# Counting the experts in use: sums of the dense gates on GpSimd, or products of one-hots on TensorE

## The chip, the cores and the metric

The kernel runs on one core of a Trainium2 chip. Its time is device microseconds for one execution, the median of several. Five engines work side by side, each through its own list of instructions in order: TensorE (PE; its weight loads are shown as PEld), VectorE (DVE), ScalarE (ACT), GpSimd (POOL) and SyncE (SP), which issues transfers. They wait for each other by semaphores. TensorE writes to PSUM, in banks of 128x512 fp32; SBUF holds the rest.

## The reference, cut to what matters

One layer works on 256 latent tokens of width 2048 (with 256 context tokens that only the first half of the layer reads): a token mixer, and then an expert layer (PEER), which is where the change lies.

```
q  = (hb @ w_q).reshape(128, 8 heads, 2, 128)
s1, s2 = q[:, :, 0] . k1, q[:, :, 1] . k2              # 128 scores each
v1, i1 = top_k(s1, 16);  v2, i2 = top_k(s2, 16)
sc, flat = top_k(v1[:, None] + v2[None, :], 16)        # 16 pairs for each token and head
idx = e1 * 128 + e2                                    # one of 16384 experts
g   = softmax(sc)
act = gelu(hb . u_tab[idx])
out = sum over the 128 (head, k) of (g * act) * v_tab[idx]
```

Each token picks 8 x 16 experts. An expert is one row of u_tab and one of v_tab, of 2048 fp32 each.

## The kernel before, in words

**Stages.** Up to about 600 us: modulation, norm, the mixer and its output projection, then the queries and scores of the expert layer. From there to about 1380 us runs the u stage: 128 steps (`u_step`, L1181), one for each tile of 128 experts of u_tab. All 16384 experts are computed for all 256 tokens. A step has 16 pairs of matmuls (L1188, L1190) into one of four banks. Each u tile comes by DMA and is split into a high and a low part, in two halves of 1024 columns: ScalarE rounds (L255), VectorE subtracts (L256). Five half buffers let these splits be made two tiles ahead of their step. From the eighth step on ScalarE copies the bank out (L1203), GpSimd adds its two halves (L1204), and in the next step ScalarE applies the GeLU (L1209) and stores the activations to DRAM. Then comes the v stage: rows of v_tab in use are gathered by index and multiplied.

**What is done beneath the u stage.** `beneath` (L1160) is a generator of small pieces of work. In each u step `fill` takes pieces from it until their given costs use up a budget of 3000; what is left over or overdrawn is carried on. So the order on each engine is settled by the program, not by what is free at the time. In a u step it is: the splits, the u matmuls, the pieces, the GeLU of the step before, the copy out. The pieces are routing (top-k and softmax), `gates`, `places` and `make_list`.

**Gates.** The gates are spread into a dense table G[e2, e1, token]: expert (e1, e2) has partition e2 and column e1. This is done in 32 blocks of 8 tokens (TB); for tokens of a half (NB = 16 blocks). Partitions hold the 128 (head, k) slots. For each block VectorE makes one-hots of e2 (OHA) and of e1 (both L1025), and multiplies those of e1 by the gate's high and low fp16 parts (L1034). A block later TensorE multiplies, for each of 8 tokens, the e2 one-hot by both scaled e1 one-hots (L1057, two matmuls into banks 6 and 7: G for 4 tokens in each), and the e2 one-hot by the plain e1 one-hot (L1054), which counts how often each expert is picked: bank 4 for the first 128 tokens, bank 5 for the others, accumulated over 16 blocks. A block later again `keep` has ScalarE copy banks 6 and 7 to the dense table GC in SBUF (L1067, four tokens each). GC holds 64 tokens in 128 columns of 64, so the four tokens of one copy are 128 runs of four numbers. Finished tables go to DRAM (`agd`) in pieces.

**Places.** After the last block VectorE compares both counts with 0.5 (L1093, L1094), which tells which experts the first half, the second or both use. From this the list of v rows is made.

Of the kernel before, what the change touches and what calls it, by code (L numbers as in the profile page):

```python
# [14 lines left out]
ALU = mybir.AluOpType  # L15
AX = mybir.AxisListType

P = 128
# [32 lines left out]
def layer_kernel(ctx: ExitStack, tc: tile.TileContext, I, out, dbg=None):  # L51
    nc = tc.nc
    V, S, G, TE = nc.vector, nc.scalar, nc.gpsimd, nc.tensor
# [11 lines left out]
    pb = [psum.tile([P, 512], F32, name=f"bank{i}") for i in range(8)]  # L65

    def q_(off, n):
        assert O_Q + off + n <= N_F
        return fa[:, O_Q + off:O_Q + off + n]
# [793 lines left out]
    TB = 8  # L863
    NB = P // TB
# [5 lines left out]
    GC = [a.rearrange("p (c t) -> p c t", t=HT) for a in (fb[:, 0:8192], q_(0, 8192))]  # L870
# [4 lines left out]
    PM, PJ = q_(11264, 64).bitcast(BF), q_(11328, 64).bitcast(BF)  # L875
    VAL = q_(11392, 128).bitcast(F16).rearrange("p (n q) -> p n q", q=2)
    PT = [q_(11520, 128)] + [q_(12288 + 128 * i, 128) for i in range(4)]
    STAGE = [q_(12032, 256), q_(14976, 256), dg2]
    eg = q_(14336, 512)
    E1T, E2T = eg[:, 0:128].bitcast(BF), eg[:, 128:256].bitcast(BF)  # L880
# [131 lines left out]
    def list_tables():  # L1012
# [5 lines left out]
        V.tensor_scalar(VAL[:, :, 1], iota_f, 0.0, pidx, op0=ALU.mult, op1=ALU.add)  # L1018
        V.memset(PT[0], 0.0)
        S.dma_start(agd[0:1, :].rearrange("a (b c) -> (a b) c", c=P), PT[0][0:4, :])  # L1020
        yield 1000


    def one_hot(dst, numbers, n):
        V.tensor_tensor(dst, iota_b[:, 0:n].unsqueeze(1).to_broadcast([P, TB, n]),  # L1025
                        numbers.unsqueeze(2).to_broadcast([P, TB, n]), op=ALU.is_equal)

    def pair(b, n):
        return (OHB[b % 2][:, 0:TB * n].rearrange("p (t j) -> p t j", t=TB),
                OHG[b % 2][:, 0:2 * TB * n].rearrange("p (t q j) -> p t q j", t=TB, q=2))  # L1030

    def scaled(b, factors, n):
        oj, og = pair(b, n)
        V.tensor_tensor(og, oj.unsqueeze(2).to_broadcast([P, TB, 2, n]),  # L1034
                        factors.unsqueeze(3).to_broadcast([P, TB, 2, n]), op=ALU.mult)
# [5 lines left out]
    def store_piece(eng):  # L1041
        if pieces:
            c, x = pieces.pop(0)
            cs = slice(8 * x, 8 * x + 8)
            eng.dma_start(ag4[cs, :, c // 2, 1, (c % 2) * HT:(c % 2 + 1) * HT].rearrange("c e i -> e c i"),
                          GC[c % 2][:, cs, :])

    def gates():
        def products(b):
            counts = pb[4 + b // NB][:, 0:P]  # L1050
            oj, og = pair(b, P)
            for i in range(TB):
                oa = OHA[b % 2][:, i, :]
                TE.matmul(counts, oa, oj[:, i, :], start=b % NB == 0 and i == 0,  # L1054
                          stop=b % NB == NB - 1 and i == TB - 1, skip_group_check=True)
                for q in range(2):
                    TE.matmul(pb[6 + i // 4][:, (i % 4) * P:(i % 4 + 1) * P], oa, og[:, i, q, :],  # L1057
                              start=i % 4 == 0 and q == 0, stop=q == 1, skip_group_check=True)

        def keep(b):  # L1060
            c, o = divmod(b, HT // TB)
            if o == 0:
                while pieces and pieces[0][0] < c - 1:
                    store_piece(S)
            for x in range(2):
                tl = slice(o * TB + 4 * x, o * TB + 4 * x + 4)
                S.activation(GC[c % 2][:, :, tl], pb[6 + x].rearrange("p (t j) -> p j t", j=P), AF.Copy,  # L1067
                             scale=1.0 / GSC)
            if o == HT // TB - 1:
                pieces.extend((c, x) for x in range(16))  # L1070

        for b in range(2 * NB + 2):
            sl = slice(b * TB, (b + 1) * TB)
            if b < 2 * NB:
                one_hot(OHA[b % 2], E2T[:, sl], P)
                one_hot(pair(b, P)[0], E1T[:, sl], P)
            yield 2300
            if b < 2 * NB:
                scaled(b, GT[:, sl, :], P)
            if b > 1:  # L1080
                keep(b - 2)
            if 0 < b <= 2 * NB:
                products(b - 1)
            yield 2400
# [3 lines left out]
    def places():  # L1088
        flat = [o.rearrange("p t i -> p (t i)")[:, 0:P].bitcast(BF) for o in OHA]
        u0, u1 = flat[0], flat[1]  # L1090
        part = [x[:, 0:P].bitcast(BF) for x in (OHB[0], OHB[1], OHG[1])]
        one, tot, inc, pos = PT[0], PT[1], PT[2], PT[3]
        V.tensor_scalar(u0, pb[4][:, 0:P], 0.5, None, op0=ALU.is_gt)  # L1093
        V.tensor_scalar(u1, pb[5][:, 0:P], 0.5, None, op0=ALU.is_gt)  # L1094
        V.tensor_tensor(part[1], u0, u1, op=ALU.mult)
        V.tensor_tensor(part[0], u0, part[1], op=ALU.subtract)
        V.tensor_tensor(part[2], u1, part[1], op=ALU.subtract)
        yield 1500
        for x in range(3):
            TE.matmul(pb[6][:, x * P:(x + 1) * P], LT, part[x], start=x == 0, stop=True, skip_group_check=True)  # L1100
            TE.matmul(pb[7][:, x * P:(x + 1) * P], ONES, part[x], start=x == 0, stop=True, skip_group_check=True)
        V.memset(one, 1.0)
        V.memset(pos, BIG)
        yield 500

        for x in range(3):
            V.tensor_copy(tot, pb[7][:, x * P:(x + 1) * P])
            V.tensor_tensor_scan(inc, one, tot, 0.0, op0=ALU.mult, op1=ALU.add)
            V.tensor_tensor(tot, inc, tot, op=ALU.subtract)
            V.tensor_tensor(tot, pb[6][:, x * P:(x + 1) * P], tot, op=ALU.add)  # L1110
            if x == 0:
                V.tensor_scalar(flag[:, 0:1], inc[:, P - 1:P], float(N_A * P), None, op0=ALU.is_gt)
                V.tensor_scalar(PT[4], tot, float(N_A * P) - 0.5, BIG, op0=ALU.is_gt, op1=ALU.mult)
                V.tensor_tensor(tot, tot, PT[4], op=ALU.add)
            else:
                base = float(N_A * P) if x == 1 else flag[:, 1:2]
                V.tensor_scalar(tot, tot, base, None, op0=ALU.add)
                V.tensor_scalar(flag[:, x:x + 1], inc[:, P - 1:P], base, None, op0=ALU.add)
            V.scalar_tensor_tensor(tot, tot, -BIG, part[x], op0=ALU.add, op1=ALU.mult)
            V.tensor_tensor(pos, pos, tot, op=ALU.add)  # L1120
            yield 2200
        V.tensor_scalar(flag[:, 1:2], flag[:, 1:2], float(N_0 * P), None, op0=ALU.is_gt)
        V.tensor_scalar(flag[:, 2:3], flag[:, 2:3], float(N_L * P), None, op0=ALU.is_gt)
        G.dma_start(ptab.rearrange("(p c) a -> p (c a)", p=P), pos)
        pu, pj = PT[4].bitcast(U32), PT[0].bitcast(U32)
        V.tensor_copy(pu, pos)
        V.tensor_scalar(pj, pu, 7, None, op0=ALU.logical_shift_right)
        V.tensor_copy(PJ, pj)
        V.tensor_scalar(pu, pu, P - 1, None, op0=ALU.bitwise_and)
        V.tensor_copy(PM, pu)  # L1130
        yield 2500
# [28 lines left out]
    def beneath():  # L1160
        yield from routing()
        yield from list_tables()
        yield from gates()
        yield from places()
        yield from make_list()
        while pieces:
            yield 0
        for n in range(N_RAW):
            yield from (0 for _ in starts(NU - 16 + 3 * n))
            gather(n)  # L1170
            yield 100
# [9 lines left out]
    def u_step(n, fill):  # L1181
# [15 lines left out]
        u_out(n - 1)  # L1197
        st = STAGE[n % 3]
        if n < 8:
# [6 lines left out]
    def u_out(n):  # L1206
        if n >= 0:
            st = STAGE[n % 3]
            S.activation(st, st, AF.Gelu_apprx_tanh)  # L1209
            S.dma_start(ag4[n, :, :, 0, :], st.rearrange("p (t i) -> p t i", t=2))  # L1210
# [80 lines left out]
    with tc.If(more > 0):  # L1291
# [23 lines left out]
        for t in range(2):  # L1315
# [9 lines left out]
            for q in range(4):  # L1325
                c = slice(q * 512, (q + 1) * 512)
# [163 lines left out]
```

## Time and profile before

| | |
|---|---|
| time, median of 3 runs (lowest to highest) | 1791.05 us (1789.89 to 1794.6) |
| the profiled execution: its time, its span | 1794.17 us, 1792.4 us |
| mean granted TensorE clock | 0.982 of full speed |
| busy share: TensorE, VectorE, ScalarE, GpSimd | 95%, 75%, 51%, 22% |
| u stage with gate products | 778 to 1106 us |

Busy time of an engine adds up its instructions; an instruction that has been issued and waits for something inside its engine is shown as busy. "L256" is line 256 of the kernel. In a group `out<-in` are the buffers by the program's names (`fa`, `fb`: large fp32 buffers in SBUF; `ra`: the rounded parts; `bank`: PSUM), followed by partitions x elements, type and the number of instructions. A wait is shown with the engine, buffer and line that ended it.

### The profile page before, as it was taken

The numbers are of one execution on the slowest core, as the hardware profiler recorded it, in microseconds if no ns is written. First come the engines' busy times: TensorE is split into PE (matmuls) and PEld (weight loads), VectorE is DVE, ScalarE is ACT, GpSimd is POOL, SyncE is SP. The second block draws the span as 40 slices with busy tenths as digits, with TensorE's granted clock in tenths as the row PEclk, the third lists the DMA queues.
The fourth block names the chain that finished last, engine by engine and source line by source line (L and its number), as shares of the span: only waits on it lengthen the run. The fifth ranks groups of instructions, "written<-read, shape, count | busy, mean of one in ns | idle before, by whom it ended". The sixth has DMA issues, their size and how long they took to land.

```text
span 1792.4 us, 26487 instructions
## 1 busy us (share of the span) xinstructions
PE 1707.9 (95%) x10313; PEld 1422.4 (79%) x10313; DVE 1340.4 (75%) x1812; ACT 922.0 (51%) x1232; POOL 401.5 (22%) x341
## 2 busy tenths in 40 slices
PE   4999999999999999999999999999998799999995
PEld 0778566788799888888888888888887688888884
DVE  1347697687788999898888886988443577777776
ACT  5223666643543455555555555444454465656554
POOL 0000000000100002222222221212112565656652
PEclk8999999999999999999999999999999899999997
DMA  9877778888797656655787888865675789888881
GB/s 394 335 307 281 297 274 323 329 322 299 291 338 283 242 202 215 209 187 184 220 236 227 226 242 235 260 216 189 213 276 189 247 307 350 309 304 307 305 315 59
DMA packets 166266, 472.43 MB, mean 264 GB/s; under 512 B 76692, under 2 KB 109640, under 8 KB 115960
## 3 DMA queue, kind: packets, MB, share of 16 engines
q1 hardware_dynamic: 92544, 316.17, 50.3%
q0 software_dynamic: 21120, 128.68, 20.3%
q10 hardware_dynamic: 52472, 25.84, 5.0%
q8 instruction: 82, 1.34, 0.3%
q14 instruction: 48, 0.39, 0.1%
HBM read 432.81 MB, written 37.83 MB: 263 GB/s over the span
## 4 chain that ended last, share of the span: by engine, by line
PE 80%; DVE 11%; DMA 5%; issue 2%; ACT 2%; POOL 0%; SPq 0%; DVEq 0%; POOLq 0%; ACTq 0%
PE bank L1188 23%; PE bank L284 13%; PE bank L286 12%; PE bank L285 12%; PE bank L1190 12%; DVE ra L256 4%; DMA fa<-in_wm_a_dram 2%; DMA fa<-in_wm_c_dram 2%; PE bank L1057 2%; PE bank L364 1%; PE bank L309 1%; DVE fa L290 1%; DVE fa L942 1%; PE bank L527 1%; DVE fa L940 1%
## 5 line engine op out<-in xcount | busy, mean ns | idle before, releaser
L256 DVE TENSOR_TENSOR ra<-fa,ra 128x1024 fp32r<-128x1024 f32 x564 | 702.0, 1259 | 291.9 <-ACT ra L255 286.2
L255 ACT ACTIVATE ra<-fa 128x1024 fp32r<-128x1024 f32 x564 | 591.3, 1057 | 473.7 <-PE bank L1188 187.3
L1188 PE MATMUL bank<-ra 128*128 128x512 f32 x2048 | 731.9, 401 | 0.0
L1190 PE MATMUL bank<-ra 128*128 128x256 f32 x2048 | 576.9, 282 | 5.1 <-DVE ra L256 5.0
L284 PE MATMUL bank<-ra 128*128 128x512 f32 (+1 forms) x1364 | 475.0, 348 | 17.9 <-ACT ra L1229 16.8
L286 PE MATMUL bank<-ra 128*128 128x512 f32 (+1 forms) x1364 | 468.2, 343 | 5.4 <-DVE ra L1234 4.5
L285 PE MATMUL bank<-ra 128*128 128x512 f32 (+1 forms) x1364 | 467.8, 343 | 1.4 <-DVE ra L256 1.4
L1188 PEld LDWEIGHTS bank<-ra 128*128 128x128 f32 x2048 | 385.8, 188 | 92.6 <-ACT ra L255 0.2
L1190 PEld LDWEIGHTS bank<-ra 128*128 128x128 f32 x2048 | 387.7, 189 | 8.5 <-DVE ra L256 8.4
L284 PEld LDWEIGHTS bank<-ra 128*128 128x128 f32 x1364 | 261.8, 192 | 76.7 <-issue 25.8
L1204 POOL TENSOR_TENSOR fa<-fa 128x256 f32<-128x256 f32 x120 | 150.9, 1258 | 724.2 <-ACT fa L1203 724.1
L286 PEld LDWEIGHTS bank<-ra 128*128 128x128 f32 x1364 | 261.5, 192 | 36.7 <-DVE ra L1234 6.5
L285 PEld LDWEIGHTS bank<-ra 128*128 128x128 f32 x1364 | 261.8, 192 | 32.1 <-DVE ra L256 3.1
L1203 ACT ACTIVATE fa<-bank 128x512 f32<-128x512 f32 x120 | 71.8, 598 | 145.8 <-PE bank L1190 139.8
L898 POOL DMA_INDIRECT fa<-agd,fa x92 | 128.3, 1395 | 39.1 <-issue 26.5
L898 POOL DMA_INDIRECT fa<-in_peer_v_dram,fa x92 | 97.4, 1058 | 119.8 <-DVE ra L256 80.1
L1025 DVE TENSOR_TENSOR fa<-fa 128x1024 f16<-128x1024 bf16 x96 | 113.5, 1223 | 0.0
L1034 DVE TENSOR_TENSOR fa<-fa 128x2048 f16<-128x2048 f16 (+1 forms) x48 | 109.2, 2275 | 0.8
L290 DVE SCALAR_TENSOR_TENSOR fa<-fa 128x2048 f32<-128x2048 f32 x32 | 72.9, 2284 | 0.0
L1209 ACT ACTIVATE fa<-fa 128x256 f32<-128x256 f32 x128 | 52.0, 407 | 33.7 <-DVE fa L1201 25.6
L364 PE MATMUL bank<-fa 128*2 128x512 f32 x256 | 39.6, 711 | 25.5 <-DMA fa<-in_wm_a_dram 17.4
L1229 ACT ACTIVATE ra<-fa 128x128 fp32r<-128x128 f32 x92 | 32.4, 352 | 50.9 <-DVE fa L1220 50.7
(264 smaller groups left out, 1168.1 us busy)
## 6 DMA issues: line engine op xcount, KB each, us to landing
fa<-in_peer_u_dram SPq DMA_DIRECT2D x128, 1024.0 KB, 5.1
fa<-in_wm_a_dram SPq DMA_DIRECT2D x32, 1024.0 KB, 7.8
fa<-in_wm_c_dram SPq DMA_DIRECT2D x32, 1024.0 KB, 6.8
fa<-in_wm_d_dram SPq DMA_DIRECT2D x32, 1024.0 KB, 6.8
fa<-in_w_in_dram SPq DMA_DIRECT2D x24, 1024.0 KB, 4.9
fa<-in_w_out_dram SPq DMA_DIRECT2D x16, 1024.0 KB, 6.7
fa<-in_wq_dram SPq DMA_DIRECT2D x16, 1024.0 KB, 7.4
agd<-fa ACTq DMA_DIRECT2D x128, 128.0 KB, 2.4
```

The costliest lines, as they stand in the source:

```text
L255: S.activation(h, x, AF.Copy)
L256: V.tensor_tensor(l, x, h.bitcast(F32), op=ALU.subtract)
L284: TE.matmul(dst, wh, mh, start=first, stop=False, skip_group_check=skip)
L285: TE.matmul(dst, wh, ml, start=False, stop=False, skip_group_check=skip)
L286: TE.matmul(dst, wl, mh, start=False, stop=last, skip_group_check=skip)
L290: V.scalar_tensor_tensor(junk, w, 1.0, s, op0=ALU.mult, op1=ALU.mult, accum_out=dst)
L898: G.indirect_dma_start(out=dst, out_offset=None, in_=src, in_offset=bass.IndirectOffsetOnAxis(ap=idx, axis=0), bounds_check=bound, oob_is_ ...
L1025: V.tensor_tensor(dst, iota_b[:, 0:n].unsqueeze(1).to_broadcast([P, TB, n]), numbers.unsqueeze(2).to_broadcast([P, TB, n]), op=ALU.is_equal)
L1034: V.tensor_tensor(og, oj.unsqueeze(2).to_broadcast([P, TB, 2, n]), factors.unsqueeze(3).to_broadcast([P, TB, 2, n]), op=ALU.mult)
L1188: TE.matmul(bank, h[:, es], H2[:, k, :, :].rearrange("p z t -> p (z t)"), start=k == 0, stop=False, skip_group_check=True)
L1190: TE.matmul(bank[:, 0:T], l[:, es], HH[:, k, :], start=False, stop=k == KD - 1, skip_group_check=True)
L1204: G.tensor_tensor(st, HALVES[:, 0:T], HALVES[:, T:2 * T], op=ALU.add)
```

## The change

TensorE no longer counts. After each `keep` GpSimd adds the two freshly copied quarters of the dense table to a running sum SUMS (128 columns x 4), two additions of 128x512 for each block, one in the first block of each half. After the sixteenth block of a half VectorE reduces SUMS over its last axis to USED (128x128), and `places` compares USED with zero. A used expert has a positive gate. What is left of `places` and all other stages are unchanged, and lines move by up to 8.

```diff
+    SUMS = q_(12288, 512).rearrange("p (j t) -> p j t", t=4)
+    USED = [q_(11648 + 128 * i, 128) for i in range(2)]
...
         def products(b):
-            counts = pb[4 + b // NB][:, 0:P]
             oj, og = pair(b, P)
             for i in range(TB):
                 oa = OHA[b % 2][:, i, :]
-                TE.matmul(counts, oa, oj[:, i, :], start=b % NB == 0 and i == 0,
-                          stop=b % NB == NB - 1 and i == TB - 1, skip_group_check=True)
                 for q in range(2):
...
+            quarter = [GC[c % 2][:, :, o * TB + 4 * x:o * TB + 4 * x + 4] for x in range(2)]
+            if b % NB == 0:
+                G.tensor_tensor(SUMS, quarter[0], quarter[1], op=ALU.add)
+            else:
+                for x in range(2):
+                    G.tensor_tensor(SUMS, SUMS, quarter[x], op=ALU.add)
+            if b % NB == NB - 1:
+                V.tensor_reduce(USED[b // NB], SUMS, axis=AX.X, op=ALU.add)
...
-        V.tensor_scalar(u0, pb[4][:, 0:P], 0.5, None, op0=ALU.is_gt)
-        V.tensor_scalar(u1, pb[5][:, 0:P], 0.5, None, op0=ALU.is_gt)
+        V.tensor_scalar(u0, USED[0], 0.0, None, op0=ALU.is_gt)
+        V.tensor_scalar(u1, USED[1], 0.0, None, op0=ALU.is_gt)
```

TensorE at the first products, before (bank_78 takes the counts, bank_80 the gates):

```order
L1188 MATMUL bank_76<-ra 128x512
L1190 MATMUL bank_76<-ra 128x256
L1054 LDWEIGHTS fa
L1054 MATMUL bank_78<-fa 128x128
L1057 LDWEIGHTS fa
L1057 MATMUL bank_80<-fa 128x128
L1057 LDWEIGHTS fa
L1057 MATMUL bank_80<-fa 128x128
L1054 LDWEIGHTS fa
```

The same place now (u matmuls are L1196 and L1198, gate products L1056):

```order
L1196 MATMUL bank_76<-ra 128x512
L1198 MATMUL bank_76<-ra 128x256
L1056 LDWEIGHTS fa
L1056 MATMUL bank_80<-fa 128x128
L1056 LDWEIGHTS fa
L1056 MATMUL bank_80<-fa 128x128
L1056 LDWEIGHTS fa
```

A count went with its own weight load: three loads and three matmuls for each token have become two and two.

GpSimd's list in the u stage, before (L1204 is the addition of a u step):

```order
L1204 TENSOR_TENSOR fa<-fa 128x256
L726 DMA m5d<-fa 16x128
L1204 TENSOR_TENSOR fa<-fa 128x256 x18
L1013 IOTA fa 128x1
L1204 TENSOR_TENSOR fa<-fa 128x256 x57
L1124 DMA ptab<-fa 128x128
```

And now (L1212 is what L1204 was, L1071 and L1074 are the new additions):

```order
L1015 IOTA fa 128x1
L1212 TENSOR_TENSOR fa<-fa 128x256 x4
L1071 TENSOR_TENSOR fa<-fb 128x512
L1212 TENSOR_TENSOR fa<-fa 128x256 x2
L1074 TENSOR_TENSOR fa<-fa,fb 128x512 x2
L1212 TENSOR_TENSOR fa<-fa 128x256
L1074 TENSOR_TENSOR fa<-fa,fb 128x512 x2
L1212 TENSOR_TENSOR fa<-fa 128x256 x2
```

Two new additions stand ahead of the u step's own in each step that keeps a block.

VectorE at the end of the first half, now (L1027 one-hots, L1036 scaled one-hots, L256 splits; L1076 waits for GpSimd):

```order
L256 TENSOR_TENSOR ra<-fa,ra 128x1024 x2
L1027 TENSOR_TENSOR fa<-fa 128x1024 x2
L256 TENSOR_TENSOR ra<-fa,ra 128x1024 x2
L1036 TENSOR_TENSOR fa<-fa 128x2048
L1076 TENSOR_REDUCE fa<-fa 128x128
L256 TENSOR_TENSOR ra<-fa,ra 128x1024 x2
L1027 TENSOR_TENSOR fa<-fa 128x1024 x2
```

Apart from L1076, here and once more ahead of `places`, VectorE's list is what it was.

## Rows read from the trace of the kernel before

**Rows 1.** The page, busy us (share of the span) xinstructions.
```profile
PE 1707.9 (95%) x10313; PEld 1422.4 (79%) x10313; DVE 1340.4 (75%) x1812; ACT 922.0 (51%) x1232; POOL 401.5 (22%) x341
```
**Rows 2.** The page, chain that ended last, shares of the span by line.
```profile
PE bank L1188 23%; PE bank L284 13%; PE bank L286 12%; PE bank L285 12%; PE bank L1190 12%; DVE ra L256 4%; DMA fa<-in_wm_a_dram 2%; DMA fa<-in_wm_c_dram 2%; PE bank L1057 2%; PE bank L364 1%; PE bank L309 1%; DVE fa L290 1%; DVE fa L942 1%; PE bank L527 1%; DVE fa L940 1%
```
**Rows 3.** Stretches: length, busy of PE, PEld, DVE, ACT, POOL (x), PEclk, DMA, GB/s.
```profile
778.00:1091.00 313.00, 313.00 (x2270) 273.76 (x2269) 275.48 (x189) 167.48 (x250) 76.13 (x48) 1.00 0.76 220
1091.00:1106.00 15.00, 15.00 (x103) 13.10 (x102) 5.92 (x5) 8.90 (x14) 1.47 (x2) 1.00 0.86 233
```
**Rows 4.** Groups, 778 to 1106 us: xcount | busy us, mean ns | idle before.
```profile
L256 DVE TENSOR_TENSOR ra<-fa,ra 128x1024 fp32r<-128x1024 f32 x102 | 140.7, 1390 | 46.4 <-ACT ra L255 46.3
...
L1204 POOL TENSOR_TENSOR fa<-fa 128x256 f32<-128x256 f32 x50 | 77.6, 1552 | 249.2 <-ACT fa L1203 249.2
L1025 DVE TENSOR_TENSOR fa<-fa 128x1024 f16<-128x1024 bf16 x61 | 75.1, 1270 | 0.0
L1034 DVE TENSOR_TENSOR fa<-fa 128x2048 f16<-128x2048 f16 x31 | 74.4, 2399 | 0.2
```
**Rows 5.** VectorE's timeline in the u stage: start us, us, instruction.
```profile
817.89 2.29 DVE L1034 TENSOR_TENSOR fa<-fa 128x2048 f16<-128x2048 f16 x1
820.17 1.68 DVE L256 TENSOR_TENSOR ra<-fa,ra 128x1024 fp32r<-128x1024 f32 x1
```
**Rows 6.** GpSimd's timeline at the same time.
```profile
819.27 1.50 POOL L1204 TENSOR_TENSOR fa<-fa 128x256 f32<-128x256 f32 x1 [3.86 <-ACT fa L1203]
```
**Rows 7.** By line, whole span: ns min/median/max, first and last start us, forms.
```profile
L256 DVE TENSOR_TENSOR ra<-fa,ra x564: 1164/1225/1765, 37.7 to 1773.7; 128x1024 fp32r<-128x1024 f32 x188
L1025 DVE TENSOR_TENSOR fa<-fa x96: 909/1217/1762, 764.5 to 1247.5; 128x1024 f16<-128x1024 bf16 x80, 128x736 f16<-128x736 bf16 x16
L1034 DVE TENSOR_TENSOR fa<-fa x48: 1691/2285/2823, 770.1 to 1248.4; 128x2048 f16<-128x2048 f16 x32, 128x1472 f16<-128x1472 f16 x16
L776 DVE TENSOR_TENSOR fa<-bank,fa x8: 678/684/692, 469.4 to 479.1; 128x512 f32<-128x512 f32 x8
L777 POOL TENSOR_TENSOR fb<-fa,fb x4: 1283/1292/1296, 470.2 to 474.0; 128x512 f32<-128x512 f32 x4
L777 DVE TENSOR_TENSOR fb<-fa,fb x4: 692/692/1447, 474.4 to 479.8; 128x512 f32<-128x512 f32 x4
L1371 POOL TENSOR_TENSOR fb<-fb,fa x7: 1267/1277/1290, 1749.9 to 1782.6; 128x512 f32<-128x512 f32 x7
L1204 POOL TENSOR_TENSOR fa<-fa x120: 727/1470/2683, 653.2 to 1384.6; 128x256 f32<-128x256 f32 x120
```
**Rows 8.** Timelines of GpSimd and VectorE, 468 to 482 us.
```profile
470.24 5.04 POOL L777 TENSOR_TENSOR fb<-fa,fb 128x512 f32<-128x512 f32 x4 [80.34 <-ACT fa L757]
...
474.39 1.45 DVE L777 TENSOR_TENSOR fb<-fa,fb 128x512 f32<-128x512 f32 x1
```
**Rows 9.** TensorE's timeline, starts of three u steps and of one block's products.
```profile
799.95 0.48 PE L1188 MATMUL bank<-ra 128*128 128x512 f32 x1
...
805.68 0.23 PE L1054 MATMUL bank<-fa 128*128 128x128 f16 x1
...
807.00 0.48 PE L1188 MATMUL bank<-ra 128*128 128x512 f32 x1
...
812.74 0.40 PE L1188 MATMUL bank<-ra 128*128 128x512 f32 x1
```
**Rows 10.** L1067 in a stretch: length, ACT busy (x), PEclk, DMA, GB/s.
```profile
778.00:1091.00 313.00, 32.00 (x60) 1.00 0.76 220
```
**Rows 11.** VectorE's timeline behind the last scaled one-hots; in brackets idle before.
```profile
1099.33 1.22 DVE L256 TENSOR_TENSOR ra<-fa,ra 128x1024 fp32r<-128x1024 f32 x1 [2.41 <-ACT ra L255]
```
**Rows 12.** ScalarE's timeline, a keep and a later GeLU.
```profile
836.41 1.06 ACT L1067 ACTIVATE fb<-bank 128x512 f32<-128x512 f32 x2
...
843.46 0.40 ACT L1209 ACTIVATE fa<-fa 128x256 f32<-128x256 f32 x1
```
**Rows 13.** A stretch ahead of the u stage, columns as in rows 3.
```profile
300.00:400.00 100.00, 96.64 (x708) 79.73 (x708) 82.15 (x83) 56.23 (x64) 2.61 (x5) 0.98 0.83 321
```

## The prediction

> **What bounds the kernel now.** I read the page's busy line first: TensorE is busy 95% of the span, VectorE 75%, GpSimd 22% [rows 1]. In the chain that ended last the expert-u stage's matmuls (L1188, L1190) alone make 35% [rows 2]. The removed products are L1054, so the stage to look at is where they run, 778 to 1106 us. By stretches: from 778 to 1091 us TensorE is busy for all of the 313.0 us, VectorE for 275.5 and GpSimd for 76.1 [rows 3]. TensorE sets the pace there, and VectorE has 37.5 us of slack, 12%. That is the number on which everything turns.
>
> What VectorE does there, by groups [rows 4]: 102 splits of u tiles (L256), 61 one-hots (L1025), 31 scaled one-hots (L1034). All of them read two operands from SBUF. GpSimd does one addition of 128x256 per u step (L1204, 50 of them). The two engines disturb each other, which the reader can see in any step: L1034 ends at 817.89 + 2.29 = 820.18, the GpSimd addition that was issued at 819.27 then runs to 820.77, and the split that VectorE has next (L256 at 820.17) takes 1.68 us and not the 1.23 of its line's median [rows 5 to 7]. GpSimd waited for VectorE's instruction, and VectorE's next one waited for GpSimd. Over the window: (1390-1225) ns x 102 + (1270-1217) x 61 + (2399-2285) x 31 = 23.5 us, means from the window against the medians of the lines [rows 4, 7], by 50 additions: 0.47 us of VectorE for each 128x256 addition. A VectorE instruction with one operand in PSUM shows none of it: L776 stayed at 678 to 692 ns beside four GpSimd additions [rows 7, 8].
>
> **What goes from TensorE.** Of 24 small matmuls per block of 8 tokens, 8 go; weights of each are loaded anew, so no load stays behind. A step with products lasts from 799.95 to 807.00, the next one, without, from 807.00 to 812.74; the 24 stand between 805.68 and 807.00, 55 ns each [rows 9]. 32 blocks x 8 x 55 ns = 14.1 us. They lie on the path, so by themselves they would be worth 14.1 us.
>
> **What comes to GpSimd.** For each of 32 blocks two additions of 128x512 (one in the first block of each half): 62. The keeps (L1067) run 60 times from 778 to 1091 us, so 30 blocks and 58 additions fall there [rows 10], where VectorE is loaded; 4 fall behind. GpSimd's only rows of that size are L777 (1.28 to 1.30 us) and L1371 (1.27 to 1.29), dense operands, and an undisturbed 128x256 takes 0.73 [rows 7]. GpSimd has room: 58 x 1.29 = 75 us beside 76. What matters is what each takes from VectorE. Scaled from the small one: 0.47 + (1.28 - 0.73) = 1.02 us. Checked on the last L777 of GpSimd: the four end at 475.28, and VectorE's L777, begun at 474.39, takes 1.45 us against 0.69 [rows 7], so it was let go 0.76 us later, 0.13 us before GpSimd's record ends, 1.16 us after that addition began [rows 8]. I take 1.05: 58 x 1.05 = 60.9 us. [...]
>
> **What comes to VectorE.** Two reductions of 128x512, about 0.69 us each (the nearest row is L777 on VectorE [rows 7]), and a wait for the last two additions before each. The first stands in the loaded stretch, and the splits and one-hots of the next steps are queued behind it; additions already counted run meanwhile, so I charge 0.7 + 1. The second comes when VectorE idles. The comparisons (L1093, L1094) read SBUF in place of PSUM: nothing, two instructions.
>
> **The sum.** From 778 to 1091 us VectorE needs 275.5 + 60.9 + 1.7 = 338.1 us and TensorE only 313 - 13.6 = 299.4. VectorE becomes the bound and the stretch has to grow by 25.1 us, less what VectorE may fall behind before TensorE notices. Splits are made two tiles ahead; products are the tighter tie, since those of a block stand one block behind its scaled one-hots. Where both fall in neighbouring steps, as at 817.89, the values are ready at 820.18, at the start of a step, and wanted after its 5.7 us of u matmuls [rows 5, 9]: some 5.3 us of lag. This is paid back behind 1091 us, where VectorE idles 9.1 of 15 us [rows 3]. 25.1 - 5.3 = 19.8 us. A step with one-hots alone needs 4 x 1.22 + 0.47 = 5.4 us of VectorE [rows 7], less than TensorE's 5.7, so it won't be filled perfectly: 3 us more. Total +23 us. The profiled execution took 1794.17 us (span 1792.4), 3 over the median 1791.05; on the median's footing 1791 + 23 = **1814 us**.
>
> Bounds of the unknown term, the VectorE time that one strided 128x512 addition takes: 0.47 us (as a 128x256) gives 275.5 + 27.3 + 1.7 = 304.5, no bound any more; 2.6 us (two whole dense ones) gives 428 and +110. The break-even is (313 + 5.3 - 277.2) / 58 = 0.71 us; the nearest row, 1.02 to 1.16, lies above it.
>
> **Rivals.**
> 1. *The additions fit into VectorE's slack; the kernel is faster.* Decided at 0.71 us per addition. For it: 37.5 us of slack, and GpSimd idles 249 us there [rows 4]. Against it: slack lies before splits, in pieces up to 2.4 us [rows 11], but each addition starts when its keep ends, whatever VectorE does then. With nothing lost, 1791 - 14 = 1777; between 0.61 and 0.80 us, no change.
> 2. *The strided reads are slower than dense ones.* Each addition reads 128 runs of 4 elements, 64 apart; no addition of GpSimd in these rows does. If a 128x512 of this kind took VectorE 1.6 us, half more: 275.5 + 92.8 + 1.7 = 370, less 313 and 5.3, +52 and 3: 1846; at 2.1 us +84, 1875. For it: nothing in the trace; against it: the runs are dense inside, and one of the two operands is dense throughout, so a whole second stream's cost is the far end. [...]
> 3. *GpSimd's queue becomes the late one.* L1204 now stands behind two additions, and ScalarE's L1209 of the next step waits for it, with the copy L1203 and the splits' L255 behind it in ScalarE's order. At 837.47 (the end of a keep) two additions and an L1204, each behind a split of 1.22 us, need 2 x (1.22 + 1.29) + 1.22 + 0.73 = 7.0 us, to 844.4, and L1209 is due about 843.5 [rows 12]. 0.9 us late in each of 31 blocks, 28 us on top of the forecast's 23, if none of it hid: 1842. VectorE, late itself, would hide most of it.
> 4. *TensorE's clock.* It was granted 1.00 here; at 96% busy (300 to 400 us) it was 0.98 [rows 13]. 2% of 300 us is 6 us, inside the range, and VectorE would cover it.
>
> **Chances.** The forecast's case (0.8 to 1.35 us per addition, +5 to +45) 0.62; rival 2 0.20; rival 3 0.05; rival 1, faster 0.07, and its in-between case 0.06. The range leaves out rival 1's gain and the far end of rival 2: 1796 to 1866; the likeliest case alone gives 1800 to 1832. About 0.3%, 5.4 us, can be told from no change: faster 0.07, within 0.06, slower 0.87.
>
> **What would show it.** The first product of a block to the first matmul of the next step shrinks from 1.32 to 0.88 us. From 778 us on VectorE's busy share rises from 88% towards 100%, L256, L1025 and L1034 have higher means, TensorE shows idle time ended by VectorE (before the products and the u matmuls), and the stretch is some 20 us longer in the end. GpSimd's new lines have a mean over 1.29 us, as waits are in it. Stages before 778 and behind 1113 us keep their lengths. I am wrong if VectorE's lines keep their means beside the additions, if TensorE stays busy throughout, or if its idle time is ended by ScalarE.

## The result and the profile after

The changed kernel takes 1814.15 us (median of 4 runs, 1812.83 to 1817.0) against 1792.01 us for the kernel before on the same chip (1789.89 to 1794.6): 1.0139 times as long, 95% interval 1.0109 to 1.0168 (the quotient of the two medians, 1.0124, lies inside it). The profiled execution took 1813.66 us, with a span of 1811.8. In the page's busy line VectorE and GpSimd have risen and TensorE has fallen, and in the chain that ended last the u matmuls (L1196 and L1198 now) have fallen from 35% to 31%, while VectorE's share has risen from 11% to 14%, with the scaled one-hots (L1036) new among its lines [rows 1, 2]:

```profile
PE 1704.4 (94%) x10057; PEld 1414.1 (78%) x10057; DVE 1403.7 (77%) x1814; ACT 922.9 (51%) x1232; POOL 549.8 (30%) x403
...
PE 75%; DVE 14%; DMA 6%; issue 3%; ACT 1%; POOL 0%; SPq 0%; DVEq 0%; POOLq 0%; ACTq 0%
PE bank L1196 21%; PE bank L284 12%; PE bank L286 12%; PE bank L285 12%; PE bank L1198 10%; DVE ra L256 5%; DMA fa<-in_wm_a_dram 2%; DVE fa L1036 2%; PE bank L1056 2%; PE bank L527 1%; PE bank L309 1%; PE bank L364 1%; DMA fa<-agd,fa 1%; DVE fa L290 1%; DMA fa<-in_wm_c_dram 1%
```

The stretches of [rows 3] again (length, busy time of TensorE, its weight loads, VectorE, ScalarE and GpSimd with instructions, granted clock, DMA share, GB/s), and two short ones inside:

```profile
778.00:1091.00 313.00, 290.61 (x1895) 252.22 (x1894) 311.29 (x176) 159.13 (x238) 200.57 (x99) 0.96 0.69 205
...
820.00:837.00 17.00, 12.54 (x82) 10.64 (x80) 17.00 (x10) 9.30 (x14) 13.42 (x7) 0.99 0.57 187
837.00:850.00 13.00, 12.94 (x77) 11.44 (x78) 13.00 (x11) 5.00 (x8) 2.27 (x3) 0.89 0.50 181
```

The two engines have changed places: VectorE is busy for 311.3 of 313 us, TensorE for 290.6, where it was busy throughout. In the groups of 778 to 1130 us (instructions, busy us, mean ns, idle time before with what ended it) the splits take 1621 ns and not 1390, the one-hots 1765 and not 1270, the scaled one-hots 2772 and not 2399 [rows 4]; GpSimd's new additions stand at 2063 and 2179 ns:

```profile
L256 DVE TENSOR_TENSOR ra<-fa,ra 128x1024 fp32r<-128x1024 f32 x102 | 161.7, 1621 | 5.1 <-ACT ra L255 2.8 <-DMA agd<-fb 2.2
...
L1027 DVE TENSOR_TENSOR fa<-fa 128x1024 f16<-128x1024 bf16 x60 | 103.6, 1765 | 0.0
L1212 POOL TENSOR_TENSOR fa<-fa 128x256 f32<-128x256 f32 x50 | 93.7, 1874 | 80.3 <-ACT fa L1211 80.3
L1036 DVE TENSOR_TENSOR fa<-fa 128x2048 f16<-128x2048 f16 x31 | 85.9, 2772 | 0.2
L1074 POOL TENSOR_TENSOR fa<-fa 128x512 f32<-128x512 f32 x32 | 66.0, 2063 | 24.8 <-ACT fa L1066 23.5
L1074 POOL TENSOR_TENSOR fa<-fa,fb 128x512 f32<-128x512 f32 x28 | 61.0, 2179 | 18.2 <-ACT fb L1066 17.1
```

The waits of the same window (engine and line waiting, what ended it; us in total, times, longest):

```profile
PE bank L1056 <- DVE fa L1036: 24.8, 8, 5.2
...
DVE fa L1076 <- POOL fa L1074: 3.8, 2, 2.6
...
ACT fa L1217 <- POOL fa L1212: 3.3, 7, 0.8
```

All of TensorE's idle time there (24.8 us) was ended by a scaled one-hot of VectorE (L1036), at the products, as the tighter of the two ties. It came in eight waits of up to 5.2 us, seven of them longer than half a microsecond and 35 to 57 us apart. TensorE's timeline shows one such stop (start, us, instructions; idle time in brackets), after one of the products that came in time:

```profile
794.60 1.07 PE L1056 MATMUL bank<-fa 128*128 128x128 f16 x16
795.48 0.48 PE L1196 MATMUL bank<-ra 128*128 128x512 f32 x1
...
837.06 1.89 PE L1056 MATMUL bank<-fa 128*128 128x128 f16 x16 [4.53 <-DVE fa L1036]
838.71 0.78 PE L1196 MATMUL bank<-ra 128*128 128x512 f32 x1
839.28 0.41 PE L1198 MATMUL bank<-ra 128*128 128x256 f32 x1
```

In time, a block's 16 products last from 794.60 to 795.48, 0.88 us. At 837.06 they come 4.5 us late and take 1.65 us, and the first u matmul behind them 0.78 us in place of 0.48: the granted clock was 0.51 from 837 to 840 us, so the stretch of 837 to 850 us has 0.89. VectorE and GpSimd at that time:

```profile
829.75 3.99 DVE L256 TENSOR_TENSOR ra<-fa,ra 128x1024 fp32r<-128x1024 f32 x2
833.66 3.35 DVE L1036 TENSOR_TENSOR fa<-fa 128x2048 f16<-128x2048 f16 x1
836.93 2.87 DVE L1027 TENSOR_TENSOR fa<-fa 128x1024 f16<-128x1024 bf16 x2
839.73 2.35 DVE L256 TENSOR_TENSOR ra<-fa,ra 128x1024 fp32r<-128x1024 f32 x2
```

```profile
831.32 3.54 POOL L1074 TENSOR_TENSOR fa<-fa,fb 128x512 f32<-128x512 f32 x2 [0.90 <-ACT fb L1066]
834.82 2.77 POOL L1212 TENSOR_TENSOR fa<-fa 128x256 f32<-128x256 f32 x1
845.87 1.28 POOL L1212 TENSOR_TENSOR fa<-fa 128x256 f32<-128x256 f32 x1 [8.28 <-ACT fa L1211]
```

While GpSimd has additions to do, two splits take 3.99 us and a scaled one-hot 3.35. While TensorE stands (832.5 to 837.1 us) no new block is kept. So GpSimd has nothing to add just behind the stop (8.28 us idle, from 837.6 us), and VectorE runs undisturbed: two splits in 2.35 us. The debt grows for several u steps and is paid in one stop.

From the start of the 29th u step to that of the 83rd, which holds all products, TensorE's timeline gives 351.3 us before and 373.3 after. Elsewhere: from the 83rd to the 128th step 264.9 us in both, from there to the end (the last u step and the v stage) 414.3 and 414.9, and the stages ahead of the products ended 3.1 us sooner in the profile after. With 22.0 and +0.6, less 3.1, the two profiled executions differ by their 19.5 us (1813.66 and 1794.17); the products' stretch is the one that changed. By TensorE's own account: 14.1 us of counts gone, 24.8 us of stops, and about 12 us from the lower clock (an estimate from 0.96 over 313 us): +22.7. The stretch before and after, with the columns of above:

```profile
761.80:1113.20 351.40, 351.02 (x2506) 306.63 (x2504) 300.04 (x223) 189.28 (x283) 82.87 (x55) 1.00 0.76 220
...
758.70:1132.00 373.30, 348.19 (x2249) 301.85 (x2247) 362.73 (x225) 190.13 (x283) 228.00 (x116) 0.96 0.69 207
```

VectorE's busy time has grown by 62.7 us and its idle time has shrunk from 51.4 to 10.6 us; what the idle time did not take up is the 22 us.

### The profile page after: what moved, and what is told of

Read it like the earlier page. It is cut to its first block, busy times and chain, and to the rows that moved or that the text cites. A ratio compares the mean times of both kernels' runs of the same rounds, so it can differ in the third digit from the quotient of the medians.

```text
span 1811.8 us, 26103 instructions
## 1 busy us (share of the span) xinstructions
PE 1704.4 (94%) x10057; PEld 1414.1 (78%) x10057; DVE 1403.7 (77%) x1814; ACT 922.9 (51%) x1232; POOL 549.8 (30%) x403
## 4 chain that ended last, share of the span: by engine, by line
PE 75%; DVE 14%; DMA 6%; issue 3%; ACT 1%; POOL 0%; SPq 0%; DVEq 0%; POOLq 0%; ACTq 0%
PE bank L1196 21%; PE bank L284 12%; PE bank L286 12%; PE bank L285 12%; PE bank L1198 10%; DVE ra L256 5%; DMA fa<-in_wm_a_dram 2%; DVE fa L1036 2%; PE bank L1056 2%; PE bank L527 1%; PE bank L309 1%; PE bank L364 1%; DMA fa<-agd,fa 1%; DVE fa L290 1%; DMA fa<-in_wm_c_dram 1%
## 5 line engine op out<-in xcount | busy, mean ns | idle before, releaser
L256 DVE TENSOR_TENSOR ra<-fa,ra 128x1024 fp32r<-128x1024 f32 x564 | 722.9, 1301 | 247.2 <-ACT ra L255 238.9
L1196 PE MATMUL bank<-ra 128*128 128x512 f32 x2048 | 737.4, 404 | 0.0
L1198 PE MATMUL bank<-ra 128*128 128x256 f32 x2048 | 579.1, 283 | 5.1 <-DVE ra L256 5.0
L1196 PEld LDWEIGHTS bank<-ra 128*128 128x128 f32 x2048 | 389.4, 190 | 93.3 <-ACT ra L255 0.2
L1198 PEld LDWEIGHTS bank<-ra 128*128 128x128 f32 x2048 | 391.1, 191 | 8.4 <-DVE ra L256 8.2
L1212 POOL TENSOR_TENSOR fa<-fa 128x256 f32<-128x256 f32 x120 | 166.4, 1387 | 551.5 <-ACT fa L1211 551.3
L900 POOL DMA_INDIRECT fa<-agd,fa x92 | 132.6, 1441 | 39.6 <-issue 26.5
L1027 DVE TENSOR_TENSOR fa<-fa 128x1024 f16<-128x1024 bf16 x96 | 143.8, 1537 | 0.0
L1036 DVE TENSOR_TENSOR fa<-fa 128x2048 f16<-128x2048 f16 (+1 forms) x48 | 120.3, 2507 | 0.8
L1074 POOL TENSOR_TENSOR fa<-fa 128x512 f32<-128x512 f32 x32 | 66.0, 2063 | 24.8 <-ACT fa L1066 23.5
L290 DVE SCALAR_TENSOR_TENSOR fa<-fa 128x2048 f32<-128x2048 f32 x32 | 72.9, 2285 | 0.0
L1074 POOL TENSOR_TENSOR fa<-fa,fb 128x512 f32<-128x512 f32 x28 | 61.0, 2179 | 18.2 <-ACT fb L1066 17.1
```

The lines of the kernel that those rows point to most:

```text
L256: V.tensor_tensor(l, x, h.bitcast(F32), op=ALU.subtract)
L900: G.indirect_dma_start(out=dst, out_offset=None, in_=src, in_offset=bass.IndirectOffsetOnAxis(ap=idx, axis=0), bounds_check=bound, oob_is_ ...
L1074: G.tensor_tensor(SUMS, SUMS, quarter[x], op=ALU.add)
L1196: TE.matmul(bank, h[:, es], H2[:, k, :, :].rearrange("p z t -> p (z t)"), start=k == 0, stop=False, skip_group_check=True)
L1198: TE.matmul(bank[:, 0:T], l[:, es], HH[:, k, :], start=False, stop=k == KD - 1, skip_group_check=True)
L1212: G.tensor_tensor(st, HALVES[:, 0:T], HALVES[:, T:2 * T], op=ALU.add)
```

## The experiments

Each ran beside the kernel before on the same chip, and its time is given as a ratio to that. The ratio is not the quotient of the medians beside it; in each row that quotient lies within the interval. "Stretch" is the time from the 29th to the 83rd u step in the one profiled execution. These executions are not all typical: that of e5 was the fastest of seven (1776.76 us). In stretches that TensorE bounds, up to 5 us come from a slightly different pace of the u matmuls (last section).

| kernel | median / before, us | ratio [95%] | stretch, us |
|---|---|---|---|
| before | | | 351.3 |
| after | 1814.15 / 1792.01 | 1.0139 [1.0109, 1.0168] | 373.3 |
| e1 no sums | 1776.03 / 1788.1 | 0.9931 [0.9908, 0.9954] | 336.9 |
| e2 counts and sums | 1811.03 / 1788.1 | 1.0129 [1.0106, 1.0152] | 372.7 |
| e3 writes only | 1771.93 / 1788.1 | 0.9910 [0.9889, 0.9930] | 331.6 |
| e4 dense reads | 1811.43 / 1788.1 | 1.0129 [1.0109, 1.0150] | 371.9 |
| e5 half width | 1781.29 / 1787.32 | 0.9955 [0.9937, 0.9973] | 339.7 |
| e6 VectorE adds | 1787.86 / 1787.32 | 1.0000 [0.9985, 1.0014] | 346.1 |
| e7 VectorE reduces | 1782.67 / 1787.32 | 0.9965 [0.9943, 0.9987] | 340.8 |
| e8 shared count | 1781.37 / 1787.32 | 0.9964 [0.9946, 0.9982] | 339.8 |
| e9 GpSimd copies | 1810.35 / 1789.47 | 1.0119 [1.0091, 1.0147] | 368.4 |

The rows of e1 to e9 below are of the stretch 775 to 1088 us, with the columns of the stretches above, or groups and waits of 764 to 1120 us.

**e1: no counts, no sums.** The used experts come from a fixed list, so that the later stages do about as much work.

```diff
+        V.tensor_scalar(USED[0], iota_f, 65.0, None, op0=ALU.is_lt)
+        V.tensor_scalar(USED[1], iota_f, 26.0, None, op0=ALU.is_ge)
+        V.scalar_tensor_tensor(USED[1], iota_f, 90.0, USED[1], op0=ALU.is_lt, op1=ALU.mult)
...
-                G.tensor_tensor(SUMS, quarter[0], quarter[1], op=ALU.add)
...
-                    G.tensor_tensor(SUMS, SUMS, quarter[x], op=ALU.add)
...
-                V.tensor_reduce(USED[b // NB], SUMS, axis=AX.X, op=ALU.add)
```

Expected:

> The changed kernel without the sums: TensorE doesn't count, GpSimd adds nothing, VectorE reduces nothing; which experts are in use is a fixed pattern of columns, of about as many experts, so the lists are not those of the gates. It shows what taking the counts from TensorE is worth by itself. All theories: VectorE needs the 275.5 us it needed before, TensorE 299, so TensorE bounds again and 14 us go from the kernel before: 1792 - 14 = 1778 us. Theory A (what GpSimd's additions take from VectorE is the loss): the whole distance to the changed kernel's 1814, 36 us, is theirs. If this kernel stays above 1785, the counts were not on the path, and A has less to explain.

```profile
775.00:1088.00 313.00, 313.00 (x2112) 271.85 (x2110) 281.70 (x194) 175.20 (x262) 77.36 (x50) 1.00 0.80 231
```

TensorE is busy throughout again, and the stretch is 14.4 us shorter than before, where the 256 counts of 55 ns gave 14.1. So the loss comes with the sums alone.

**e2: counts and sums.** The counting products run again, and `places` reads them; the sums run too and are used by nothing.

```diff
+            counts = pb[4 + b // NB][:, 0:P]
...
+                TE.matmul(counts, oa, oj[:, i, :], start=b % NB == 0 and i == 0,
+                          stop=b % NB == NB - 1 and i == TB - 1, skip_group_check=True)
...
-        V.tensor_scalar(u0, USED[0], 0.0, None, op0=ALU.is_gt)
+        V.tensor_scalar(u0, pb[4][:, 0:P], 0.5, None, op0=ALU.is_gt)
```

Expected:

> The changed kernel with the counts back on TensorE: both ways run, the list is made from the counts, the sums and their reductions are made and not read. Theory A (VectorE with GpSimd's additions bounds the stretch): VectorE's work is that of the changed kernel, and TensorE's 14 us more fit into its 25 us of idle time: 1814 us, at most 1819. Rival B (each addition costs the path something by a wait in a queue, L1212 or the reduction, and TensorE's work adds to that): 1814 + 14 = 1828.

```profile
775.00:1088.00 313.00, 297.89 (x2117) 260.48 (x2115) 312.76 (x176) 158.22 (x237) 192.97 (x100) 0.98 0.69 203
...
PE bank L1059 <- DVE fa L1036: 17.6, 9, 3.3
```

14.1 us of TensorE's work came back and the time did not move (372.7 against 373.3). The room for it came about half from the stops, 17.6 us in place of 24.8, and about half from the clock, 0.98 in place of 0.96. A cost that merely adds to TensorE's would have given 14 us more. With VectorE as the bound, these 14 us of TensorE's work are free, and so is its lower clock.

**e3: writes only.** Four memsets of 128x512 by GpSimd for each block in place of the sums; fixed list as in e1.

```diff
-                G.tensor_tensor(SUMS, quarter[0], quarter[1], op=ALU.add)
...
+            for x in range(4):
+                G.memset(SUMS, float(x))
```

Expected:

> In place of the additions of a block GpSimd runs four fills of 128x512 of the same buffer, which write SBUF and read nothing, about as long as two additions if a fill takes some 0.5 us; fixed pattern of experts in use, no reductions. The instructions stand at the same place in GpSimd's list, after the same keep. Theory A in the form that two instructions that both read two SBUF operands exclude each other: VectorE's L256, L1027 and L1036 return to the means of before (1390, 1270, 2399 ns), 1778 us. Rival B (GpSimd's queue is late, L1212 and with it ScalarE): GpSimd is as late as in the changed kernel, 1800 us or more. If any GpSimd instruction excludes VectorE's, writing too, VectorE's means stay high (1600 and more for L256) and the time is between 1795 and 1815.

```profile
775.00:1088.00 313.00, 313.00 (x2141) 273.91 (x2140) 283.07 (x195) 179.01 (x267) 147.31 (x179) 1.00 0.81 236
...
L256 DVE TENSOR_TENSOR ra<-fa,ra 128x1024 fp32r<-128x1024 f32 x118 | 157.0, 1348 | 32.3 <-ACT ra L255 32.3
L1073 POOL MEMSET fa<- 128x512 f32 x128 | 67.2, 525 | 5.5
```

128 memsets, 67 us of GpSimd, and the splits have the mean of e1 (1348 against 1346 ns over the same window), as have the one-hots (1338 against 1343) and the scaled ones (2358 against 2360). In this run GpSimd's being busy and its writes took nothing from VectorE; its reads are what is left for the price. The run was 5 us shorter in the stretch than e1, which neither theory had: most of its u steps were 0.10 us shorter, with the same matmuls (last section).

**e4: dense reads.** The additions read 512 neighbouring numbers, so the sums mean nothing; their reductions go to a spare buffer, and the list is fixed.

```diff
-            quarter = [GC[c % 2][:, :, o * TB + 4 * x:o * TB + 4 * x + 4] for x in range(2)]
+            quarter = [GC[c % 2].rearrange("p j t -> p (j t)")[:, 512 * x:512 * x + 512].rearrange("p (j t) -> p j t", t=4) for x in range(2)]
```

Expected:

> The additions read 512 neighbouring numbers of the table in place of 128 runs of four, so they sum the wrong ones; the reductions go to a spare buffer, and the pattern of experts in use is fixed. Theory A with the cost of dense rows (1.05 us of VectorE each): no difference to the changed kernel, 1814 us, means of the additions 2.06 to 2.18 us as there. Rival C (the strided reads are slower than dense ones, and the price came out at 1.05 by something else): each addition takes VectorE at least 0.2 us less, 12 us in all, 1802 or below.

```profile
775.00:1088.00 313.00, 290.66 (x1919) 253.45 (x1918) 309.26 (x177) 161.24 (x239) 197.74 (x99) 0.96 0.69 204
...
L1077 POOL TENSOR_TENSOR fa<-fa 128x512 f32<-128x512 f32 x32 | 62.4, 1949 | 30.0 <-ACT fa L1069 28.7
L1077 POOL TENSOR_TENSOR fa<-fa,fb 128x512 f32<-128x512 f32 x28 | 59.1, 2111 | 19.9 <-ACT fb L1069 18.8
```

The two groups are of 778 to 1130 us, as those of the kernel after. Dense reads make no difference to the time (1.0129 against 1.0139, intervals overlapping) and 114 and 68 ns to the means of the additions (2063 and 2179 ns there), in which waits are. Runs of four numbers cost nothing that decides.

**e5: half the width.** The same number of additions, over the first 64 columns only; reduced to a spare buffer, fixed list.

```diff
-            quarter = [GC[c % 2][:, :, o * TB + 4 * x:o * TB + 4 * x + 4] for x in range(2)]
+            quarter = [GC[c % 2][:, 0:64, o * TB + 4 * x:o * TB + 4 * x + 4] for x in range(2)]
```

Expected:

> The sums take only the first 64 of 128 columns: as many additions, at the same places, of 128x256; fixed pattern of experts in use, reductions to a spare buffer. Theory A: an addition takes from VectorE about what L1204's did, 0.5 us, and 275.5 + 58 x 0.5 + 1.5 = 306 us less 5.3 of lag is what TensorE needs anyway (299): 1776 to 1780 us, some 12 below the kernel before, so the loss has a threshold and is not by the instruction. If the loss goes by the number of additions, whatever their size (waits, handing over): 1805 or more. If it is simply proportional to size without a threshold, half of the distance between e1 and the changed kernel: 1794.

```profile
775.00:1088.00 313.00, 310.69 (x2084) 269.53 (x2083) 309.68 (x192) 174.23 (x261) 167.83 (x110) 1.00 0.79 227
...
L256 DVE TENSOR_TENSOR ra<-fa,ra 128x1024 fp32r<-128x1024 f32 x116 | 174.1, 1537 | 6.6 <-ACT ra L255 6.6
L1077 POOL TENSOR_TENSOR fa<-fa 128x256 f32<-128x256 f32 x32 | 48.7, 1523 | 36.8 <-ACT fa L1069 35.6
```

This is the other side of the break-even of 0.71 us: by the means of the three VectorE groups against [rows 7], less 0.47 us for each u addition, an addition takes an estimated 0.50 us of VectorE. VectorE is nearly as full as in the kernel after (309.7 of 313 us), yet TensorE loses only 2.3 us, of which a VectorE instruction ended 0.8, and the stretch is 2.8 us longer than without sums. A full VectorE and a kernel faster than before: the bound is a threshold, and a busy share close to 100% does not say on which side of it one stands. Its 1781.3 us lie just above the 1776 to 1780 that I had expected.

**e6: the same additions on VectorE.** Everything is computed; `sums` runs on VectorE one block after the keep.

```diff
+        def sums(b):
...
-                G.tensor_tensor(SUMS, quarter[0], quarter[1], op=ALU.add)
+                V.tensor_tensor(SUMS, quarter[0], quarter[1], op=ALU.add)
...
+            if b > 2:
+                sums(b - 3)
```

Expected:

> The same additions, on VectorE itself, one block later, so that it doesn't wait for the keep; the result is the reference's. Theory A: an addition costs VectorE its own 0.69 us (128x512, two operands in SBUF) and not the 1.05 that GpSimd's takes: 275.5 + 58 x 0.69 = 315.5 us, less 5.3, 11 us more than TensorE's 299; 1788 - 14 + 11 + 3 = 1788 us, 1780 to 1792, so better than the changed kernel by over 20 us though VectorE does more. Rival B or anything that holds GpSimd's help to be a help: worse than the changed kernel, 1811 + 58 x 0.69 = 1850.

```profile
775.00:1088.00 313.00, 304.93 (x2064) 264.93 (x2062) 311.58 (x248) 173.15 (x259) 63.73 (x49) 1.00 0.76 222
...
L1079 DVE TENSOR_TENSOR fa<-fa 128x512 f32<-128x512 f32 x32 | 25.5, 798 | 0.8
```

The surprise that the theory demanded: given to the engine that was short of time, the additions leave the kernel 1.4% faster (1.0000 against 1.0139) than on the one that had 249 us to spare. On VectorE each takes 0.80 us of it, with waits; from GpSimd 1.05 (below). If GpSimd took nothing from VectorE, moving the additions there could only have lost.

**e7: reductions of 16 tokens on VectorE.** Everything is computed.

```diff
+                V.tensor_reduce(used if first else SUMS[:, 0:32, :].rearrange("p j t -> p (j t)"), two,
+                                axis=AX.X, op=ALU.add)
+                if not first:
+                    V.tensor_tensor(used, used, SUMS[:, 0:32, :].rearrange("p j t -> p (j t)"), op=ALU.add)
```

Expected:

> VectorE reduces 16 tokens of the dense table at a time (128x128 from 128x2048, 2.3 us) and adds the result to the running one (0.3 us), 16 times; the result is the reference's. 15 x 2.55 = 38 us stand in the loaded stretch: 313.7, less 5.3, 9 us over TensorE's 299: 1786 us, 1779 to 1790. A reduction has one operand, so GpSimd's L1204 need not wait for it.

```profile
775.00:1088.00 313.00, 309.24 (x2101) 269.02 (x2100) 308.24 (x221) 174.71 (x262) 71.36 (x50) 1.00 0.79 227
...
L1077 DVE TENSOR_REDUCE fa<-fb 128x128 f32<-128x2048 f32 x8 | 18.2, 2275 | 0.0
L1080 DVE TENSOR_TENSOR fa<-fa 128x128 f32<-128x128 f32 x14 | 4.7, 333 | 0.5
```

16 reductions and 14 small additions take 41 us of VectorE where e6's additions needed 50, and TensorE lost 3.8 us at the products against 9.3. I had expected 1786 us; it took 1782.7. Nothing shows GpSimd's additions held up by a reduction: beside the reductions those of the u steps had a mean of 1395 ns (1493 in e1), and in the kernel before one that was issued at 673.24 us ended at 674.85, while VectorE's reduction L992 ran from 674.28 to 676.57.

**e8: the count shared.** TensorE counts two blocks of eight, VectorE reduces the others as in e7, and one addition per half joins them. Everything is computed.

```diff
+                if b % 8 > 5:
+                    TE.matmul(pb[4 + b // NB][:, 0:P], oa, oj[:, i, :], start=b % NB == 6 and i == 0,
+                              stop=b % NB == NB - 1 and i == TB - 1, skip_group_check=True)
...
+            if o % 2 and o < 6:
...
+            V.tensor_tensor(USED[x], pb[4 + x][:, 0:P], USED[x], op=ALU.add)
```

Expected:

> As e7, but TensorE counts one block pair of four (those at the end of each 64 tokens) and VectorE reduces the other three; the counts and sums are added ahead of the comparison; the result is the reference's. VectorE: 275.5 + 12 x 2.55 = 306, less 5.3 = 301; TensorE: 299 + 8 x 0.44 = 303. Both fit: 1788 - 10 = 1778 us, 1774 to 1784, faster than both kernels. If e7's reductions cost by waits and not by VectorE's time, no better than e7.

```profile
775.00:1088.00 313.00, 313.00 (x2161) 272.66 (x2159) 300.73 (x215) 173.51 (x262) 77.86 (x49) 1.00 0.77 229
```

In the stretch all that was expected came: TensorE is busy throughout, at 339.8 us, 11.5 less than before. In the time only 6.0 us of it show, where 10 had been expected; the v stage of the profiled run was 418 us long in place of 414, for a reason that I did not follow. It is 0.36% faster than the kernel before (0.18 to 0.54%), as e7 is, and the two can't be told apart; of the kernels that compute everything these two are the best.

**e9: copies by GpSimd.** Four copies of 128x512 for each block, one operand each, in place of the sums; fixed list.

```diff
-                G.tensor_tensor(SUMS, quarter[0], quarter[1], op=ALU.add)
...
+            for x in range(4):
+                G.tensor_copy(SUMS, quarter[x % 2])
```

Expected:

> In place of the additions of a block GpSimd makes four copies of the quarters (128x512 from the dense table to one buffer): one operand read from SBUF and not two, nothing summed; fixed pattern of experts in use, no reductions. e3 showed that fills, which read nothing, cost VectorE nothing. If any GpSimd read excludes VectorE's instructions of two SBUF operands, each copy takes its own length less some 0.2 us from VectorE: 120 copies of 0.5 us or more are 60 us, L256's mean stays at 1550 and more, and the time is 1805 or above. If it takes two read operands on GpSimd's side too, L256 returns to about 1346 ns as in e1, and the time to 1776.

```profile
775.00:1088.00 313.00, 290.50 (x1909) 253.51 (x1908) 294.70 (x179) 159.37 (x237) 248.46 (x157) 0.97 0.70 208
...
L256 DVE TENSOR_TENSOR ra<-fa,ra 128x1024 fp32r<-128x1024 f32 x106 | 154.6, 1492 | 27.0 <-ACT ra L255 27.0
L1074 POOL COPY fa<-fb 128x512 f32<-128x512 f32 x64 | 108.1, 1688 | 18.0 <-ACT fb L1069 15.0
...
L1059 PE MATMUL bank<-fa 128*128 128x128 f16 x512 | 37.4, 230 | 24.3 <-ACT fa L1069 12.7 <-ACT fb L1069 11.6
...
ACT fa L1215 <- POOL fa L1210: 93.2, 29, 5.4
```

The time is that of one theory and the rows are of neither. VectorE is not full (294.7 of 313 us), the splits have a mean between those of e1 and of after, and TensorE is stopped all the same, now by ScalarE: all 24.3 us of its waits at the products were ended by a keep (L1069). The chain is another: a copy takes 0.61 us at its shortest and 1.69 on average (those from `fb`), most likely because it waits for VectorE's instructions; four of them a block make GpSimd late, and ScalarE's GeLU (L1215) waits 93.2 us for its u addition (3.3 us in the kernel after), with the keeps behind it in ScalarE's order. From the means of the three VectorE groups against the medians of [rows 7], less 0.47 us for each u addition, a copy takes an estimated 0.30 us of VectorE. So reading with one operand takes something, less than an addition; as a test of reads alone the run fails, because it lengthened another queue.

## Why the prediction came right, step by step

**The step that decided** was 1.05 us of VectorE for each addition, above the break-even of 0.71. By the method of [rows 4, 7] the groups after give (1621 - 1225) ns x 102 + (1765 - 1217) x 60 + (2772 - 2285) x 31 = 88.4 us; less the 23.6 us of the 50 u additions (the prediction's three terms add up to that, and not to 23.5), 64.8 us by 62 additions are 1.05 us each, if a u addition still takes its 0.47 us. VectorE's busy time says nearly the same without this condition: the 62.7 us by which it grew in the stretch, less 1.4 us of the two reductions, are 0.99 us for each of the 62. e3's memsets, which read nothing, cost nothing (1348 against 1346 ns). Of GpSimd's own shortest time an addition here took 1.05 us of 1.29 from VectorE, a copy in e9 an estimated 0.30 of 0.61; why the shares differ no run shows. The 0.47 us of a 128x256 addition, taken for the lower bound, is tested by e5, at an estimated 0.50 us, which is on the far side of the break-even as it should be.

**The counts** were worth 14.1 us: e1 has 14.4 in the stretch, and a block's products shrank from 1.32 to 0.88 us [rows 9].

**The sum.** The stretch grew by 22.0 us where +23 was forecast, on 1792 where 1791 was taken. VectorE's need was right; that the sum came within 1 us is partly luck, as the terms behind it show:
- The lag of 5.3 us was the right size from a misread example. The scaled one-hots of 817.89 are ready at 820.18, but their products come only at 831.12, 10.9 us later. The tightest blocks do have 5.3 us, as the one that is ready at 798.11 + 2.28 = 800.39 and multiplied from 805.68 on [rows 9]. (That the longest stop is 5.2 us is another quantity.) Of the kernel before:

```profile
798.11 2.28 DVE L1034 TENSOR_TENSOR fa<-fa 128x2048 f16<-128x2048 f16 x1
...
831.12 0.23 PE L1054 MATMUL bank<-fa 128*128 128x128 f16 x1
```

  Nor is the lag spent once. I had a debt that grows until 5.3 us are reached and is then passed on a little in every step; in fact a stop lets VectorE catch up undisturbed, and the debt falls and grows anew over 35 to 57 us. The block behind the stop of 837.06 is ready at 842.00 + 2.28 = 844.28 and multiplied from 850.66 on, 6.4 us later.
- The 3 us for imperfect filling was a guess. VectorE idled 1.7 of 313 us. What the guess covered is not shown by any run; that it fitted is luck.
- The first reduction, at 955.5 us, waited 1.2 us where 1 was charged. The second, at 1127.7 us, waited 2.6 us. It came where VectorE idles, as forecast: splits just ahead of it had waited 1.0 to 2.2 us for ScalarE and for a transfer, and the products were done.
- The comparisons cost nothing visible: 221 ns each, 284 and 282 before.

**Rival 1** (it fits) fell with VectorE full and TensorE stopped; e5 shows that it was a real case, one halving of the width away. **Rival 2** (strided reads) is refuted by e4: runs of four with gaps between show at most 6% (2063 and 2179 ns after, 1949 and 2111 in e4, waits included), and no difference in the time. Its 1.6 us of VectorE, half more than the 1.05, no run shows for any addition. **Rival 3** (GpSimd's queue) is not what happened: ScalarE waited 3.3 us for L1212. e9 shows that its mechanism exists, at four reading instructions a block. **Rival 4** (the clock) was underrated in size, about 12 us and not 6, and right in what it said of cover: e2 had a higher clock and the same time.

**What I would have read wrongly:** TensorE's waits come in lumps, so a look at one step shows nothing. Between 788 and 797 us, for instance, the kernel after seems simply faster: the products are shorter and nothing waits.

## What to carry to other kernels

Before work is moved to GpSimd, look at what it takes from VectorE and not at GpSimd's own idle time: in this kernel an addition of two operands in SBUF, beside VectorE instructions that read two operands there, took 1.05 us of VectorE where GpSimd needs 1.29, and 0.47 where it needs 0.73. Take a share of that size, as a first estimate, from VectorE's slack in the stage, and compare the result with the cost of doing the work on VectorE itself (0.80 us an addition in e6). When the slack is of the size of the sum, work out the break-even per instruction, as the sign hangs on it. And when an engine takes over as the bound, what is saved on the one before is worth nothing: here 14 us of counts could be put back for free.

## What I had not expected

- Each of the six stops of 2.5 us or more in the kernel after has a stretch beside it in which the granted clock was about 0.5 (0.51 in the row below), three of about 3.5 us and three of about 7; some begin before the stop ends, some behind it. The stops and the clock together take 24.8 and about 12 us from TensorE. Not every stop has one: around the two short ones, 0.23 us at 912.55 and 0.55 us at 977.03, the clock was 1.00; and in e2, by an estimate from its row, TensorE stood 15.1 us at up to 3.3 us a time, so at least five times, while a clock of 0.98 leaves room for four stretches of 3.4 us. What decides it no run here shows. In this kernel VectorE is the bound and the clock is hidden, as e2 shows (0.98 in place of 0.96, and 372.7 us in place of 373.3); what it would cost in one where TensorE bounds right behind the stop was not tried. The stretch beside the stop that ended at 936.5 us, with the columns of above:

```profile
935.40:942.40 7.00, 5.94 (x29) 5.37 (x30) 7.00 (x6) 0.00 (x0) 1.58 (x1) 0.51 0.50 171
```

- GpSimd's additions (L1074) on average took 2.06 to 2.18 us, the shortest of them 1.29. The two engines held each other up: VectorE's splits beside them had a mean of 1.62 us, with a median of 1.23 in the kernel before [rows 7].
- In e3 from the fourth step of the stretch on, a u step without products took 5.63 us in place of 5.73, with the same matmuls at clock 1.00 (mean of the 128x512 matmuls 397 ns in e3, 402 in e1). Some steps of the kernel after and of e2, e4 and e6 to e9 have this pace too; the kernel before, e1 and e5 have none. No run tells why. Some fifty steps of it make the 5.3 us by which e3 lies below e1, so where TensorE is the bound, differences of that size between two stretches say nothing of the sums.
